# A two-layer decoder trunk: running sums of MLP products kept in PSUM, and per-partition scalings moved from VectorE to ScalarE

## The chip, the cores and the metric

The kernel runs on one core of a Trainium2 chip. The metric is the device time of one execution in microseconds; lower is better. The engines are called PE (TensorE; PEld is its weight load), DVE (VectorE), ACT (ScalarE), POOL (GpSimd) and SP (SyncE, which issues most DMAs).

## The reference

A residual stream x of 256 rows and 2048 columns in f32 goes through two layers. Every sub-layer normalises its input (RMSNorm with a weight per column) and adds its result back. Layer 0 attends with differential attention, layer 1 with latent attention; both then attend to 256 memory tokens and apply a squared-ReLU MLP of width 8192.

```python
def rms_norm(x, g):
    y = xf * lax.rsqrt(jnp.mean(xf * xf, axis=-1, keepdims=True) + EPS)
    return (y * g).astype(x.dtype)

# differential attention, per pair of heads
p = jax.nn.softmax(s, axis=-1)
a = p[:, :, 0] - lam * p[:, :, 1]
o = rms_norm(a @ v, subln) * (1.0 - lambda_init)

# latent attention
d = h @ wdown
c_q  = rms_norm(d[..., :512], q_norm)
c_kv = rms_norm(d[..., 512:1024], kv_norm)
...
# MLP
x = x + jnp.square(jax.nn.relu(rms_norm(x, mlp_norm) @ wup)) @ wdown
```

## The kernel before

**Precision and weights.** Every f32 operand is split into a high part (rounded to the matmul's format) and a low part (the rest), and each product is three matmuls: high x high, high x low, low x high. Weights come from HBM in tiles of 1 MB (`raw`, 7 buffers). ACT casts 128x1024 of it to `whi` (L199), DVE subtracts to get `wlo` (L200); there are four buffers of each, so the splitting runs at most four halves ahead of PE. Activations are split in the same way: `split` (L338, L339) and `halves` (L439, L440).

**Order of the work.** PE's order is written out by hand: the program keeps a clock of PE time, side tasks yield a due time, and their transposes and small matmuls are put between the weight matmuls when they are due. The order of ACT, DVE, POOL and SP comes from a scheduler that works ahead of time with a model of the durations; `urgent()` raises the priority of what it encloses. Each engine then runs its list in that order.

**Norm weights.** A chunk of 512 columns of x is transposed on PE into PSUM (`transpose4`), multiplied by the norm weight of each column, which after the transpose is one scalar per partition and 128-wide piece (`scaled`, L343, and in `Forms.feed`, L451), and split. **Softmax** (`attend4`, `probs`) takes the exponentials on ACT, the reciprocal of the row sums on DVE, and divides on DVE (L622) before PE transposes the rows. **Head norms** of the differential attention (`normed`, L735) scale each head by its inverse root mean square on DVE.

**The MLP's up projection.** For 7 of the 8 blocks of 1024 hidden columns a class `Seven` forms the 2x2 block product with seven products instead of eight. Each product p1 to p7 has two halves (x = 0, 1) of 12 matmuls of 512 columns; the inputs are sums of row blocks of the activations (`sum_of`: s1 to s4, L468) and sums of weight tiles, made on DVE (L824) or by an accumulating DMA on POOL (L816: after p3 has split its tile, POOL's DMA adds the other quarter onto the same tile, which p7 then uses). Each product has a PSUM bank `pr` of its own. Its result is copied (p1 and p5: ACT, L892) or added to earlier ones on DVE (`add`, L886), and four of the seven products finish an output: `out` takes Relu and Square on ACT (L1212, L1213), then PE transposes and `split` stores the hidden unit for the down projection.

**The planner** (`mlp_line`) interleaves the items of `Seven` with items of the other block and of the down projection (24 matmuls each). It keeps the lead of DVE's work over PE's, from costs in `vector` and `tensor`, and takes a product when the lead is not positive. During an MLP only one PSUM bank is left to the side tasks; the down projection's open sums hold four, and the products have what is left.

Of the kernel before, what the change touches and what calls it, by code (L numbers as in the profile page):

```python
# [10 lines left out]
F32 = mybir.dt.float32  # L11
# [3 lines left out]
ALU = mybir.AluOpType  # L15
# [32 lines left out]
def trunk(ctx, tc, x, xT, xT0, mem, memT, positions, gcols, gfinal, lam_vecs, consts, W, out):  # L48
# [100 lines left out]
    def give_back():  # L149
        free_banks[0] += 1  # L150

    def mmul(o, stationary, moving, start, stop):
        n = 1
        for d in moving.shape[1:]:
            n *= d
        clock[0] += max(0.11, n / 2400 + 0.0133)
        return nc.tensor.matmul(o, stationary, moving, start=start, stop=stop)  # L157

    def flip(o, src):
        clock[0] += 0.109  # L160
# [173 lines left out]
    def split(dst, t, src):  # L334
# [3 lines left out]
        nc.scalar.copy(hi, src)  # L338
        nc.vector.tensor_tensor(dst[:, 1, :n, t * P : (t + 1) * P], src, f32(hi), ALU.subtract)  # L339

    def scaled(src, cols):
        tmp = work.tile([P, 4, P], F32, tag="ev", name=nm("xg"), bufs=EVS)
        nc.vector.tensor_tensor(tmp, src, cols.unsqueeze(2).broadcast_to([P, 4, P]), ALU.mult)  # L343
        return tmp

    def transpose4(src, pt):
# [75 lines left out]
    class Forms(Stream):  # L422
# [19 lines left out]
        def feed(self, c, t, ps):  # L442
            xc = xs[t][:, c * CH : (c + 1) * CH]

            def task():
                sum_squares(self.ss[t][:, c : c + 1], xc)
                yield T_ADD
                pt = transpose4(xc, ps)
                rows = self.raw[t][:, 4 * c : 4 * c + 4]
                cols = g[:, self.gcol + 4 * c : self.gcol + 4 * c + 4]  # L450
                nc.vector.tensor_tensor(rows, pt, cols.unsqueeze(2).broadcast_to([P, 4, P]), ALU.mult)  # L451
                self.halves((t, c // 2), c % 2, rows)
                yield T_TURN

            self.form((t, c // 2)).run(task())
# [145 lines left out]
    def attend4(score_pairs, inputs, v, dst, causal, scales=(1.0, 1.0), slack=0.0):  # L601
# [4 lines left out]
        def probs(t, p, nk):  # L606


            sb = yield from side_bank()
            heads = (2 * p, 2 * p + 1)  # L610
            pr = work.tile([P, CH], F32, tag="ev", name=nm("p"), bufs=EVS)[:, : 2 * nk]
            rows = pr.rearrange("p (h k) -> p h k", k=nk)
            if nk == P:
                view = sb.rearrange("p (h a k) -> p h a k", h=2, a=2)
                scores(view, [score_pairs(h, True) for h in heads], t, False)
                nc.vector.tensor_tensor(rows, view[:, :, 1], masks(2), ALU.add)
                nc.vector.tensor_tensor(rows, rows, view[:, :, 0], ALU.add)
                pr, rs = softmax(pr, 2, pr, scales[t])
            else:
                scores(sb.rearrange("p (h k) -> p h k", k=nk), [score_pairs(h, False) for h in heads], t, causal)  # L620
                pr, rs = softmax(sb, 2, pr, scales[t])
            nc.vector.tensor_tensor(rows, rows, rs[:, :2].unsqueeze(2).broadcast_to([P, 2, nk]), ALU.mult)  # L622
            yield T_SM + slack
            nb = nk // P
            for i in range(2 * nb):
                flip(sb[:, i * P : (i + 1) * P], pr[:, i * P : (i + 1) * P])
            src = sb[:, : 2 * nk].rearrange("p (h b q) -> p h b q", h=2, b=nb)
            hi = pTs[p][:, 0, :, :nb, t * P : (t + 1) * P]
            nc.scalar.copy(hi, src)
            nc.vector.tensor_tensor(pTs[p][:, 1, :, :nb, t * P : (t + 1) * P], src, f32(hi), ALU.subtract)  # L630
            give_back()
            yield T_TURN
# [58 lines left out]
    def attend_diff(q, k, v, dst, coef, subcols):  # L691
# [34 lines left out]
        def normed(t, blocks, out):  # L726
            for b in blocks:
                yield b
            po = out[0]
            ss = small.tile([P, 2], F32, tag="ss2", name=nm("ss2"))  # L730
            for h in range(2):
                sum_squares(ss[:, h : h + 1], po[:, h * S : (h + 1) * S])
            r = rsqrt_mean(ss, 2, S)
            os = work.tile([P, CH], F32, tag="ev", name=nm("os"), bufs=EVS)
            nc.vector.tensor_tensor(  # L735
                os.rearrange("p (h d) -> p h d", h=2), po.rearrange("p (h d) -> p h d", h=2),
                r[:, 0:2].unsqueeze(2).broadcast_to([P, 2, S]), ALU.mult,
            )
            yield T_NORM
            split(dst, t, scaled(transpose4(os, po), subcols))  # L740
            give_back()
            yield T_TURN
# [58 lines left out]
    class Seven:  # L801

        ORDER = "p1 p1 p5 p5 p6 p3 p6 p3 p2 p7 p2 p7 p4 p4".split()
        A = {"p1": (0, 0), "p2": (0, 1), "p3": "s4", "p4": (1, 1), "p5": "s1", "p6": "s2", "p7": "s3"}

        def __init__(self, l, b):
# [58 lines left out]
        def products(self, a, u, copied, out):  # L867
            p, x = u
            form = a.form(self.A[p])
            need(form.tasks)  # L870
            if x == 0:
                self.banks[p] = bank("pr")
            o = self.banks[p]
            for h, (hi, lo) in enumerate(take()):
                for k in range(2):
                    kk = 4 * x + 2 * h + k
                    wh, wl = (w[:, k * CH : (k + 1) * CH] for w in (hi, lo))
                    mmul(o, form[:, 0, kk], wh, kk == 0, False)
                    mmul(o, form[:, 0, kk], wl, False, False)
                    mmul(o, form[:, 1, kk], wh, False, kk == 7)  # L880
                pump()
            if x == 0:
                return

            def add(o, p, q, op=ALU.add):
                nc.vector.tensor_tensor(o, p, q, op)  # L886

            c = copied
            if p in ("p1", "p5", "p6", "p3"):
                c[p] = work.tile([P, CH], F32, tag="ev", name=nm(p), bufs=EVS)  # L890
            if p in ("p1", "p5"):
                nc.scalar.copy(c[p], o)  # L892
            elif p == "p6":
                add(c[p], o, c["p1"])
            elif p == "p3":
                add(c[p], o, c["p5"])
                add(c[p], c[p], c["p6"], ALU.subtract)
                out(0, 1, c[p], c[p])
            elif p == "p2":
                add(c["p1"], o, c["p1"])  # L900
                out(0, 0, c["p1"], c["p1"])
            elif p == "p7":
                add(c["p6"], o, c["p6"])
                add(c["p5"], c["p5"], c["p6"], ALU.subtract)
                out(1, 1, c["p5"], c["p5"])
            else:
                add(c["p6"], o, c["p6"])
                out(1, 0, c["p6"], c["p6"])

    def mlp_line(l):  # L910

# [22 lines left out]
        def vector(item):  # L934

            if isinstance(item.of, Seven):
                p, x = item.u
                return 1 + (p in ("p5", "p6", "p2")) + x * {"p6": 0.3, "p3": 0.9, "p2": 0.6, "p7": 0.9, "p4": 0.6}.get(p, 0)
            return 1 + 0.6 * (item.u == len(item.of.all) - 1 and item.of.close)

        def tensor(item):
# [631 lines left out]
```

## Time and profile before

| what | value |
|---|---|
| median of 3 runs | 2216.66 us (2216.47 to 2217.68) |
| span of the profiled execution, first to last instruction | 2214.3 us |
| PE busy | 2201.7 us, 10559 matmuls |
| DVE busy | 1760.7 us, 1961 instructions |
| ACT busy | 1357.0 us, 1811 instructions |
| POOL busy | 134.3 us, 222 instructions |
| granted PE clock | 0.999 |
| HBM | 205 GB/s over the span |

The page gives the profiled execution's span and no other time for it; the span is 2.4 us under the median, and what lies around it (start and end of the execution) is taken to be that. Busy times are sums over the span. The windows give the busy time of each engine in a stretch, the waits name the engine and line on which an engine stood idle, and the chain of waits follows back from the last instruction what released each step.

### The profile page before, as it was taken

Reading aid. Unit: us, or ns where it says so; the run is one execution under the profiler, and the core shown is the slowest. Engines: PE = TensorE matmul, PEld = TensorE weight load, DVE = VectorE, ACT = ScalarE, POOL = GpSimd, SP = SyncE. Lnnn points to the kernel's source line nnn. Section 1 sums busy time; section 2 is a strip of 40 time slices with the busy share of each in tenths; the row PEclk is TensorE's granted clock in tenths of the full one; section 3 lists DMA queues with packets and bytes.
Section 4 is the critical chain, followed back from the end, with each engine's and each line's share of the span. In section 5 each row is a group of like instructions: output and inputs, shape, how many; then the busy total and the mean of one; then the engine's idle time right before and its main releaser. Section 6 shows DMA issues by size and latency. Waiting matters only on the chain.

```text
span 2214.3 us, 27594 instructions
## 1 busy us (share of the span) xinstructions
PE 2201.7 (99%) x10559; PEld 1846.1 (83%) x10559; DVE 1760.7 (80%) x1961; ACT 1357.0 (61%) x1811; POOL 134.3 (6%) x222
## 2 busy tenths in 40 slices
PE   9999999999999999999999999999999999999998
PEld 7888888888888888888889988888888888888886
DVE  6665757779889889889765878778988998898874
ACT  7554546666666666666655755556766666666664
POOL 1111010000000000000000411000000000000001
PEclk9999999999999999999999999999999999999999
DMA  9446555436766766875845444634767667677681
GB/s 386 156 152 228 188 194 210 166 118 209 259 203 211 254 212 215 250 218 212 251 176 178 136 152 163 247 129 156 222 234 228 210 246 228 197 259 226 195 282 57
DMA packets 69683, 454.73 MB, mean 205 GB/s; under 512 B 7984, under 2 KB 8368, under 8 KB 17584
## 3 DMA queue, kind: packets, MB, share of 16 engines
q1 hardware_dynamic: 65232, 423.09, 53.6%
q0 software_dynamic: 4032, 29.36, 7.2%
q8 instruction: 82, 1.34, 0.2%
q10 hardware_dynamic: 288, 0.52, 0.1%
q14 instruction: 49, 0.40, 0.0%
HBM read 450.85 MB, written 2.10 MB: 205 GB/s over the span
## 4 chain that ended last, share of the span: by engine, by line
PE 93%; DVE 4%; issue 1%; ACT 1%; POOL 1%; DMA 1%; POOLq 0%; ACTq 0%; DVEq 0%
PE mm L157 65%; PE pr L157 23%; PE ax L157 2%; PE ax L161 2%; DVE wlo L200 2%; PE mm L161 1%; DVE raw L824 1%; DVE unit L440 0%; DVE raw L468 0%; POOL rs L382 0%; ACT whi L199 0%; DMA raw<-in_mlp_wup_dram 0%; DVE raw L451 0%; DMA raw<-in_da_wqkv_dram 0%; DVE x L496 0%
## 5 line engine op out<-in xcount | busy, mean ns | idle before, releaser
L199 ACT CAST whi<-raw 128x1024 fp32r<-128x1024 f32 (+2 forms) x962 | 1000.4, 1041 | 715.2 <-PE mm L157 590.6
L200 DVE TENSOR_TENSOR wlo<-raw,whi 128x1024 fp32r<-128x1024 f32 (+2 forms) x962 | 1147.8, 1209 | 344.9 <-ACT whi L199 329.6
L157 PE MATMUL mm<-whi,unit 128*128 128x512 f32 (+3 forms) x4416 | 1396.2, 388 | 0.4 <-ACT unit L370 0.4
L157 PEld LDWEIGHTS mm<-whi,unit 128*128 128x128 f32 x4416 | 825.2, 188 | 161.4 <-ACT unit L370 1.5
L157 PE MATMUL mm<-wlo,unit 128*128 128x512 f32 (+3 forms) x2208 | 851.5, 386 | 1.0 <-DVE wlo L200 1.0
L157 PE MATMUL pr<-whi,unit 128*128 128x512 f32 x1568 | 505.6, 391 | 0.0
L157 PEld LDWEIGHTS mm<-wlo,unit 128*128 128x128 f32 x2208 | 415.3, 188 | 79.2 <-DVE wlo L200 3.3
L157 PEld LDWEIGHTS pr<-whi,unit 128*128 128x128 f32 x1568 | 294.4, 188 | 61.0
L157 PE MATMUL pr<-wlo,unit 128*128 128x512 f32 x784 | 305.4, 390 | 0.6 <-DVE wlo L200 0.6
L824 DVE TENSOR_TENSOR raw<-raw,raw 128x2048 f32<-128x2048 f32 x84 | 192.1, 2287 | 26.1 <-DMA raw<-in_mlp_wup_dram 25.6
L157 PEld LDWEIGHTS pr<-wlo,unit 128*128 128x128 f32 x784 | 147.3, 188 | 31.5 <-DVE wlo L200 1.4
L496 DVE TENSOR_TENSOR x<-x,mm 128x512 f32<-128x512 f32 x152 | 100.3, 679 | 9.4 <-PE mm L157 9.0
L816 POOL DMA_DIRECT2D raw<-in_mlp_wup_dram x28 | 24.6, 879 | 1094.7 <-DVE wlo L200 1094.7
L382 POOL TENSOR_TENSOR rs<-rs,mhalf 128x1 f32<-128x1 f32 (+1 forms) x28 | 26.0, 932 | 649.3 <-DVE rs L381 649.3
L338 ACT CAST unit<-ax 128x512 fp32r<-128x512 f32 x64 | 37.2, 581 | 24.4 <-PE ax L161 24.4
L886 DVE TENSOR_TENSOR p<-pr,p 128x512 f32<-128x512 f32 x70 | 47.9, 684 | 2.6 <-PE pr L157 2.6
L157 PE MATMUL mm<-unit,whi 128*128 128x256 f32 x256 | 47.1, 285 | 0.1
L161 PE MATMUL ax<-identr,p 128*128 128x128 f32 x304 | 46.2, 272 | 0.5 <-ACT unit L1434 0.5
L161 PEld LDWEIGHTS ax<-identr,p 128*128 128x128 f32 x304 | 37.7, 139 | 10.8 <-ACT unit L1434 0.9
L1212 ACT ACTIVATE p<-p,r 128x512 f32<-128x512 f32 x56 | 40.3, 720 | 9.3 <-DVE p L886 9.2
L339 DVE TENSOR_TENSOR unit<-ax,unit 128x512 fp32r<-128x512 f32 x64 | 43.7, 683 | 1.6 <-ACT unit L338 1.1
L376 ACT ACTIVATE junk<-x 128x512 bf16<-128x512 f32 x56 | 35.2, 628 | 9.4 <-DVE x L496 8.4
(161 smaller groups left out, 1053.2 us busy)
## 6 DMA issues: line engine op xcount, KB each, us to landing
raw<-in_mlp_wup_dram SPq DMA_DIRECT2D x128, 1024.0 KB, 5.0
raw<-in_mlp_wdown_dram SPq DMA_DIRECT2D x128, 1024.0 KB, 5.1
raw<-in_da_wqkv_dram SPq DMA_DIRECT2D x45, 1024.0 KB, 7.3
raw<-in_mlp_wup_dram POOLq DMA_DIRECT2D x28, 1024.0 KB, 8.1
raw<-in_da_wo_dram SPq DMA_DIRECT2D x16, 1024.0 KB, 5.0
raw<-in_ca_wkv_dram SPq DMA_DIRECT2D x16, 1024.0 KB, 5.0
raw<-in_mla_wo_dram SPq DMA_DIRECT2D x16, 1024.0 KB, 5.2
raw<-in_ca_wq_dram SPq DMA_DIRECT2D x8, 1024.0 KB, 6.9
```

The lines of the kernel that those rows point to most:

```text
L157: return nc.tensor.matmul(o, stationary, moving, start=start, stop=stop)
L161: nc.tensor.transpose(o, src, ident)
L199: nc.scalar.copy(hi, r)
L200: nc.vector.tensor_tensor(lo, r, f32(hi), ALU.subtract)
L338: nc.scalar.copy(hi, src)
L339: nc.vector.tensor_tensor(dst[:, 1, :n, t * P : (t + 1) * P], src, f32(hi), ALU.subtract)
L376: nc.scalar.activation(junk[:, : src.shape[1]], src, AF.Square, accum_out=acc)
L382: nc.gpsimd.tensor_tensor(r[:, :n], r[:, :n], mhalf.broadcast_to([P, n]), ALU.pow)
L496: nc.vector.tensor_tensor(xc, xc, ps, ALU.add)
L824: nc.vector.tensor_tensor(o, o, q, ALU.add)
L886: nc.vector.tensor_tensor(o, p, q, op)
L1212: nc.scalar.activation(r, src, AF.Relu, scale=rstd[t])
```

## The change

Four things are changed. First, `Seven`'s products share banks: p6, p7 and p4 accumulate onto the bank of p1, p3 onto that of p5; p2 keeps its own. The running sums p1, p1+p6 and p5 are copied by ACT (`kept`, urgent) on the way; three subtractions or additions per block are left on DVE, and p4's output is read by Relu straight from the bank. The order of the fourteen half products swaps p2's second half with p7's second half, and the planner's costs of DVE work are lowered. Second, norm weights are applied by ACT in four pieces of 128 columns (`gained`). Third, softmax rows are divided by ACT, a piece per head. Fourth, head norms are applied by ACT, a piece of 256 columns per head.

```diff
-    def mmul(o, stationary, moving, start, stop):
+    def mmul(o, stationary, moving, start, stop, onto=False):
...
-        return nc.tensor.matmul(o, stationary, moving, start=start, stop=stop)
+        return nc.tensor.matmul(o, stationary, moving, start=start, stop=stop, skip_group_check=onto)
...
+    def gained(dst, src, cols):
+        for k in range(4):
+            nc.scalar.activation(dst[:, k], src[:, k], AF.Copy, scale=cols[:, k : k + 1])
+
     def scaled(src, cols):
         tmp = work.tile([P, 4, P], F32, tag="ev", name=nm("xg"), bufs=EVS)
-        nc.vector.tensor_tensor(tmp, src, cols.unsqueeze(2).broadcast_to([P, 4, P]), ALU.mult)
+        gained(tmp, src, cols)
         return tmp
...
-                nc.vector.tensor_tensor(rows, pt, cols.unsqueeze(2).broadcast_to([P, 4, P]), ALU.mult)
+                gained(rows, pt, cols)
...
-            nc.vector.tensor_tensor(rows, rows, rs[:, :2].unsqueeze(2).broadcast_to([P, 2, nk]), ALU.mult)
+            for i in range(2):
+                nc.scalar.activation(rows[:, i], rows[:, i], AF.Copy, scale=rs[:, i : i + 1])
...
-            nc.vector.tensor_tensor(
-                os.rearrange("p (h d) -> p h d", h=2), po.rearrange("p (h d) -> p h d", h=2),
-                r[:, 0:2].unsqueeze(2).broadcast_to([P, 2, S]), ALU.mult,
-            )
+            for h in range(2):
+                nc.scalar.activation(os[:, h * S : (h + 1) * S], po[:, h * S : (h + 1) * S], AF.Copy, scale=r[:, h : h + 1])
...
-        ORDER = "p1 p1 p5 p5 p6 p3 p6 p3 p2 p7 p2 p7 p4 p4".split()
+        ORDER = "p1 p1 p5 p5 p6 p3 p6 p3 p2 p7 p7 p2 p4 p4".split()
+        ONTO = {"p1": "p1", "p6": "p1", "p7": "p1", "p4": "p1", "p5": "p5", "p3": "p5", "p2": "p2"}
...
-            if x == 0:
+            onto = self.ONTO[p]
+            if x == 0 and onto == p:
                 self.banks[p] = bank("pr")
-            o = self.banks[p]
+            o = self.banks[onto]
...
-                    mmul(o, form[:, 0, kk], wh, kk == 0, False)
-                    mmul(o, form[:, 0, kk], wl, False, False)
-                    mmul(o, form[:, 1, kk], wh, False, kk == 7)
+                    mmul(o, form[:, 0, kk], wh, kk == 0 and onto == p, False, onto != p)
+                    mmul(o, form[:, 0, kk], wl, False, False, onto != p)
+                    mmul(o, form[:, 1, kk], wh, False, kk == 7, onto != p)
...
-            def add(o, p, q, op=ALU.add):
-                nc.vector.tensor_tensor(o, p, q, op)
+            def kept():
+                t = work.tile([P, CH], F32, tag="ev", name=nm(p), bufs=EVS)
+                with urgent():
+                    nc.scalar.copy(t, o)
+                return t
...
-            if p in ("p1", "p5", "p6", "p3"):
-                c[p] = work.tile([P, CH], F32, tag="ev", name=nm(p), bufs=EVS)
-            if p in ("p1", "p5"):
-                nc.scalar.copy(c[p], o)
-            elif p == "p6":
-                add(c[p], o, c["p1"])
+            if p in ("p1", "p5", "p6"):
+                c[p] = kept()
             elif p == "p3":
-                add(c[p], o, c["p5"])
-                add(c[p], c[p], c["p6"], ALU.subtract)
-                out(0, 1, c[p], c[p])
+                nc.vector.tensor_tensor(c["p6"], o, c["p6"], ALU.subtract)
+                out(0, 1, c["p6"], c["p6"])
+            elif p == "p7":
+                with urgent():
+                    nc.vector.tensor_tensor(c["p5"], c["p5"], o, ALU.subtract)
+                out(1, 1, c["p5"], c["p5"])
             elif p == "p2":
-                add(c["p1"], o, c["p1"])
+                nc.vector.tensor_tensor(c["p1"], o, c["p1"], ALU.add)
                 out(0, 0, c["p1"], c["p1"])
-            elif p == "p7":
-                add(c["p6"], o, c["p6"])
-                add(c["p5"], c["p5"], c["p6"], ALU.subtract)
-                out(1, 1, c["p5"], c["p5"])
             else:
-                add(c["p6"], o, c["p6"])
-                out(1, 0, c["p6"], c["p6"])
+                out(1, 0, o, work.tile([P, CH], F32, tag="ev", name=nm(p), bufs=EVS))
...
-                return 1 + (p in ("p5", "p6", "p2")) + x * {"p6": 0.3, "p3": 0.9, "p2": 0.6, "p7": 0.9, "p4": 0.6}.get(p, 0)
+                return 1 + (p in ("p5", "p6", "p2")) + x * {"p3": 0.6, "p2": 0.6, "p7": 0.6, "p4": 0.3}.get(p, 0)
```

## The prediction

> **What bounds the kernel now.** I read the page first, then the table by windows of 40 us, the waits of TensorE (PE) and the groups by line; for single places the chain of waits and the timeline. The page's first two lines:
>
> ```profile
> span 2214.3 us, 27594 instructions
> PE 2201.7 (99%) x10559; PEld 1846.1 (83%) x10559; DVE 1760.7 (80%) x1961; ACT 1357.0 (61%) x1811; POOL 134.3 (6%) x222
> ```
>
> PE is busy 99% of the span. Because matmuls overlap, "busy" could hide slack, so I compare the issue rate in a covered stretch of the chain with a matmul's own length in the groups by form:
>
> ```profile
> 665.01 10.88 PE mm L157 x48
> L157 PE MATMUL mm<-whi,unit 128*128 128x512 f32 x4160 | 1337.1, 392 | 0.4 <-ACT unit L370 0.4
> ```
>
> 48 matmuls in 10.88 us are 0.227 us each; one lasts 0.392. So a late operand shows as idle time only after 0.165 us of it. Next, where PE is not busy at all (columns: window, length, then busy us and count for PE, PEld, DVE, ACT, POOL; granted clock, DMA share, GB/s) and for whom it waited (total us, times, longest):
>
> ```profile
> 0.00:40.00 40.00, 38.37 (x158) 28.83 (x159) 28.63 (x59) 29.00 (x50) 0.76 (x5) 1.00 0.98 373
> 520.00:560.00 40.00, 39.71 (x179) 32.35 (x178) 37.45 (x33) 26.53 (x31) 1.91 (x2) 1.00 0.69 213
> ...
> 1280.00:1320.00 40.00, 39.48 (x247) 35.20 (x246) 31.31 (x50) 22.77 (x41) 2.19 (x5) 1.00 0.49 171
> ...
> 1640.00:1680.00 40.00, 39.60 (x177) 32.44 (x176) 36.24 (x30) 25.98 (x29) 1.74 (x2) 1.00 0.63 188
> ...
> 2200.00:2240.00 40.00, 5.54 (x25) 4.26 (x23) 4.29 (x10) 4.12 (x8) 1.10 (x2) 0.90 0.15 53
> ```
>
> ```profile
> PE mm L157 <- DVE wlo L200: 1.0, 3, 0.4
> PE pr L157 <- DVE wlo L200: 0.6, 2, 0.3
> PE ax L161 <- ACT unit L1434: 0.5, 1, 0.5
> ```
>
> 1.6 us of idle lie in the first window, 8.8 us behind the last matmul; the change touches neither. Between them seven windows (the first and last stand above) are short by 2.2 us together, nearly all in the six waits named. With 0.165 us hidden in each of seven, **all that PE loses in the middle is about 3.3 us**. That is the most that any relief of another engine can return: 0.15% of the span. A measurement of this kernel can tell about 0.2%, or 4.4 us, from no change.
>
> **The change part by part.** The matmuls keep their number, sizes and operands; four products now start without clearing the bank. So PE's 2201.7 us stay, and the question is which operands come later or sooner. The work that moves, from the groups by line:
>
> ```profile
> L199 ACT CAST whi<-raw 128x1024 fp32r<-128x1024 f32 (+2 forms) x962 | 1000.4, 1041 | 715.2 <-PE mm L157 590.6
> L200 DVE TENSOR_TENSOR wlo<-raw,whi 128x1024 fp32r<-128x1024 f32 (+2 forms) x962 | 1147.8, 1209 | 344.9 <-ACT whi L199 329.6
> L886 DVE TENSOR_TENSOR p<-pr,p 128x512 f32<-128x512 f32 x70 | 47.9, 684 | 2.6 <-PE pr L157 2.6
> L886 DVE TENSOR_TENSOR p<-p,p 128x512 f32<-128x512 f32 x28 | 19.1, 683 | 0.0
> L892 ACT COPY p<-pr 128x512 f32<-128x512 f32 x28 | 16.1, 575 | 0.0
> L343 DVE TENSOR_TENSOR xg<-mm,g 128x512 f32<-128x512 f32 x24 | 15.6, 686 | 6.4 <-PE mm L161 6.4
> ...
> L343 DVE TENSOR_TENSOR xg<-ax,g 128x512 f32<-128x512 f32 x4 | 2.6, 684 | 0.1
> L451 DVE TENSOR_TENSOR raw<-mm,g 128x512 f32<-128x512 f32 x16 | 10.3, 684 | 3.3 <-PE mm L161 3.3
> L622 DVE TENSOR_TENSOR p<-p,rsum 128x512 f32<-128x512 f32 (+1 forms) x24 | 14.4, 608 | 0.0
> L735 DVE TENSOR_TENSOR os<-ax,rs 128x512 f32<-128x512 f32 x8 | 5.5, 688 | 4.7 <-POOL rs L382 4.7
> ```
>
> Off VectorE (DVE): the 98 additions of L886 shrink to 3 per block, 42 in the 14 blocks, so 56 x 0.684 = 38.3 us; the norm weights (36 of L343 in three groups, 16 of L451) 52 x 0.686 = 35.7; divisions 14.4; head norms 5.5. Together 93.9 us: DVE falls to about 1667 us.
>
> Onto ScalarE (ACT): the nearest rows for a scaled copy out of PSUM in pieces are the latent rows' evacuations:
>
> ```profile
> 1204.81 0.73 ACT L1325 ACTIVATE lat<-mm,r 128x128 f32<-128x128 f32 x2 [0.31 <-PE mm L157]
> 1219.99 0.47 ACT L1325 ACTIVATE lat<-mm,r 128x256 f32<-128x256 f32 x1
> ```
>
> Two pieces of 128 take 0.73 us, so four take up to 1.46, against 0.686 on DVE; two of 256 at most 0.94. So 52 x 1.46 = 76 us; divisions 16 x 0.94 + 8 x 0.73 = 21; head norms 8 x 0.94 = 7.5; one copy more per block (p6), 14 x 0.575 = 8. About 112 us: ACT rises to 1470 us, 66%. Neither engine becomes the bound on average; only bursts and latencies count.
>
> [...]
>
> *The new bank waits.* p6, p7 and p4 pile onto p1's bank, p3 onto p5's, so each must wait until the sum so far has been read. I worked the planner's rule through with its new costs: from the second block on, each block reads p1 p1' p5 D p5' D p6 D p3 p6' D p3' p2 D D p7 p7' p2' D D p4 p4' (a dash: second half; D: an item of the down projection). At 0.227 us a matmul, a product item is 2.7 us and D 5.4. Between the end of p5' and p3 lie D, p6, D; between p7' and p4 lie p2', D, D: 13.6 us each; the other two gaps are longer. The reader needs 0.575 us (copy) or 0.684 (subtraction). Cost: nothing, hidden by those items; uncovered it would be their length, 56 x about 0.6 = 34 us.
>
> *Latent layer, kv latent.* Here DVE's weighting goes to an ACT that is full:
>
> ```profile
> 1224.12 1.29 DVE L343 TENSOR_TENSOR xg<-ax,g 128x512 f32<-128x512 f32 x2
> 1226.28 1.17 ACT L338 CAST unit<-xg 128x512 fp32r<-128x512 f32 x2
> 1228.78 1.83 DVE L339 TENSOR_TENSOR unit<-xg,unit 128x512 fp32r<-128x512 f32 x2
> PEld mm L157 <- DVE unit L339: 0.3, 1, 0.3
> ```
>
> The unit's casts end at 1227.45 and PE already waits for the low halves, done at 1230.61. Two weightings add 2.9 us to ACT; if all goes in front, the casts end at 1230.4, the two low halves (1.4 to 1.8) at about 1232: +1.3. If ACT lets a weight cast of 1.05 pass later, +0.3. I take **+1.0**.
>
> *Divisions.* They put 0.7 to 0.9 us on ACT for 0.6 on DVE. In the latent heads DVE is the late one too:
>
> ```profile
> 1292.60 0.67 DVE L622 TENSOR_TENSOR p<-p,rsum 128x512 f32<-128x512 f32 x1
> 1293.42 0.63 PE L161 MATMUL ax<-identr,p 128*128 128x128 f32 x4 [0.52 <-ACT unit L1434]
> ```
>
> The wait of 0.52 is put down to ACT's L1434, but what waits are transposes of probabilities, and this division, held up in DVE's queue, ends only at 1293.27. Bounds -0.7 (it goes) to +4 (one us in each of four head groups); I take **0**, as the two engines are about equally full there (31.3 and 22.8 of 40 us).
>
> *First block's accumulating DMA.* In block 1 the new order is p3' p2 p7 p7' with nothing between. p7' reads the raw tile that POOL's DMA sums onto after p3':
>
> ```profile
> 554.77 0.68 DVE L886 TENSOR_TENSOR p<-pr,p 128x512 f32<-128x512 f32 x1
> 555.37 2.35 DVE L200 TENSOR_TENSOR wlo<-raw,whi 128x1024 fp32r<-128x1024 f32 x2
> 556.90 0.87 POOL L816 DMA_DIRECT2D raw<-in_mlp_wup_dram  x1 [10.22 <-DVE wlo L200]
> raw<-in_mlp_wup_dram POOLq DMA_DIRECT2D x28, 1024.0 KB, 8.1
> DMA to landing us min/median/max: 2.6/5.0/14.4
> 563.43 4.13 PE pr L157 x18
> ```
>
> It lands at 565.0; cast 1.04 and low half 1.21 make it 567.2. PE starts p7 at 563.43 (last row), ends it 2.72 later at 566.15, and needs the low half of p7' 0.23 after that: 0.8 us late. Behind the waiting cast on ACT stand the next casts and the Relu of p3's result, which nothing needs for some 10 us. The addition at 554.77 goes, which pulls the DMA 0.6 forward. I take 0.5 in each layer, **+1.0**; bounds 0, and 6 each at the longest landing of any DMA. In later blocks D, D lie between: nothing. What moves with the swap of p2' and p7': the load of p2' on SP and its addition L824 come one item later, and p7' gives its raw tile back one to four items sooner, so no load finds fewer free tiles; POOL's DMA keeps its place.
>
> *Relief of DVE bursts.* Why PE waits at 614:
>
> ```profile
> 607.12 0.68 DVE L886 TENSOR_TENSOR p<-pr,p 128x512 f32<-128x512 f32 x1
> 611.53 2.29 DVE L824 TENSOR_TENSOR raw<-raw,raw 128x2048 f32<-128x2048 f32 x1
> 613.74 4.62 DVE L200 TENSOR_TENSOR wlo<-raw,whi 128x1024 fp32r<-128x1024 f32 x4
> 490.00:500.00 10.00, 10.00 (x50) 8.34 (x49) 10.00 (x14) 6.49 (x11) 0.00 (x0) 1.00 0.41 137
> ```
>
> The wait of 0.4 (0.57 with the hidden part) is shorter than the addition at 607.12, which goes; twice, -1.1. At the entry of each MLP DVE is full from 490 on (last row) and loses eight weightings, 5.5 us: the wait of 0.3 (0.45) goes, twice, -0.9. What is late next is a weight's cast on ACT, which has about 3.5 us idle in that window. One wait near 820 follows a DMA and stays. Sum -2.0, bounds -2.5 and +3.
>
> *Sum.* +1.0 + 0 + 1.0 - 2.0 = 0.0. The profiled execution shows 2214.3 us from first to last instruction; the median of the runs is 2216.66, the 2.4 around it being start and end. So the span stays near 2214 and the time near **2216.5**.
>
> **The rivals.**
>
> *Only the relief (0.18).* All 3.3 us return and nothing new is late: 2213.4. For it: DVE is named in five of six waits. Against it: the kv latent already waits, and ACT is full there.
>
> *ScalarE's queue (0.20): slower.* Its added pieces stand in front of weight casts and low-half work. Place: the latent layer's four head groups, the kv latent, the two MLP entries. Price: four softmaxes of 0.9 us per group, half seen by PE, 4 x 1.7 = 6.8; kv 1.3; entries: two pairs of weightings in 490 to 500 add 5.8 us against 3.5 idle, half of the 2.3 seen, at two entries 2.3; relief of 2.0 kept: +8.4, 2225.1. It decides once ACT's backlog exceeds the weights that lie ahead, four halves of 1.36 us (5.4) in a run of products. For it: the row at 1226.28; against it: 34% of ACT stays idle. [...]
>
> *The accumulating DMA (0.14).* Landing 3 us later than the median, at both layers: 2 x 3.3 extra, 2222 to 2223. It speaks for it that the margin is negative already; against, that DVE is freed just before.
>
> *Faster by more than 4.4 us (0.04).* Needs more than PE's idle time in the middle; only the edges hold it, and nothing there changes.
>
> **How the numbers follow.** The forecast has 0.44: 2216.5, its own range 2214 to 2220. The range runs from 2213.2 (full relief) to 2225 (most of the ScalarE rival); outside lie the fourth rival and about half the second, some 0.15. Faster by over 0.2%: 0.04. Slower: most of the second, over half of the third, a little of the forecast: 0.28. Within: 0.68.
>
> **What would show it.** Right: PE busy again about 2202 us; L886 with 42 additions; ACT near 1460 and DVE near 1670 us; no PE wait on ACT's p copies; the wait near 614 gone; PE waiting 1 to 1.5 us on the kv unit's low half, and up to 1 us on a low half in block 1. Wrong: waits on whi (L199) in the latent heads or MLP entries, a p7' wait of several us, or the p copies among PE's waits.

## The result, and the profile after

| kernel | median | runs |
|---|---|---|
| before | 2216.66 us | 2215.57 to 2217.68, 5 runs |
| after | 2227.37 us | 2221.98 to 2228.94, 5 runs |

The medians lie 10.7 us apart, and 2227.37 is above the upper end of the range (2225.0). The ratio over all runs is 1.0042, 95% interval [1.0031, 1.0053], or 9.4 us, which is also the difference of the means (2226.1 against 2216.7). The profiled execution of after has a span of 2227.2 us against 2214.3, so 12.9 us more. The runs of after lie up to 7 us apart, those of before 2 us. The granted clock, averaged over each run of after, goes with it: 0.996 at 2228.94 us, 0.999 at 2221.98, and the other three between or level with the first. A difference of 0.003 is some 13 us at half clock and so about 6.7 us of time, an estimate.

The page of after, its first two lines:

```profile
span 2227.2 us, 27718 instructions
PE 2208.3 (99%) x10559; PEld 1852.1 (83%) x10559; DVE 1688.6 (76%) x1821; ACT 1433.1 (64%) x2097; POOL 133.8 (6%) x222
```

The same 10559 matmuls are busy for 6.6 us more (2208.3 against 2201.7), and PE's idle time is 18.9 us against 12.6, so 6.3 more. The two add up to the 12.9. Neither DVE nor ACT has become the bound.

The idle part is found in the waits of PE in after (total us, times, longest):

```profile
PE pr L157 <- DVE wlo L200: 4.3, 2, 2.2
PE ax L161 <- ACT p L627: 2.7, 2, 2.0
PE mm L157 <- DVE unit L339: 1.4, 1, 1.4
```

These 8.4 us of idle time are new. The six waits of before that the prediction named, 2.1 us, are gone, which leaves the 6.3. The three lines are the low halves of a product (first MLP block of each layer), the divided probabilities of the latent heads, and the kv latent.

The busy part is found with the windows of after, cut at the starts of the stretches with a lower clock (window, length, busy us and count for PE, PEld, DVE, ACT, POOL; granted clock, DMA share, GB/s):

```profile
566.72:570.14 3.42, 1.24 (x8) 0.83 (x7) 3.42 (x3) 2.68 (x4) 0.00 (x0) 1.00 0.46 192
570.14:573.55 3.41, 3.41 (x9) 2.65 (x10) 3.41 (x4) 1.05 (x1) 0.00 (x0) 0.50 0.80 250
1232.32:1235.74 3.42, 1.94 (x14) 1.50 (x14) 3.42 (x5) 3.12 (x7) 3.34 (x5) 1.00 0.30 117
1235.74:1239.15 3.41, 3.41 (x18) 3.41 (x18) 1.78 (x3) 0.33 (x2) 2.96 (x5) 0.50 0.47 125
1396.16:1399.58 3.42, 1.41 (x8) 0.73 (x7) 3.42 (x9) 3.42 (x8) 0.00 (x0) 1.00 0.00 0
1399.58:1402.99 3.41, 3.41 (x12) 2.73 (x12) 0.98 (x2) 1.45 (x4) 0.00 (x0) 0.50 0.77 228
1614.62:1618.03 3.41, 1.32 (x6) 1.05 (x6) 3.41 (x4) 1.62 (x3) 0.00 (x0) 1.00 0.29 50
1618.03:1621.45 3.42, 3.42 (x9) 2.45 (x8) 3.42 (x5) 1.05 (x1) 0.00 (x0) 0.50 0.90 323
```

Each odd row holds a wait; in each even row, right after it, **PE was granted half its clock for 3.41 us**: in the first, 9 matmuls of 512 columns where 3.41 / 0.227 = 15 would fit. By the granted clock of 0.50 a stretch costs about 3.41 / 2 = 1.7 us, an estimate, and four of them 6.8; the busy time rose by 6.6. A wait of about 2 us was thus paid nearly twice, and the second payment is not in the table of waits.

How the first of these waits arises, which ends at 569.96, is shown by the chain of waits of after (start, us, what) and, under it, by DVE's timeline:

```profile
558.22 1.24 DVE wlo L200
...
559.47 6.99 DMA raw<-in_mlp_wup_dram
...
566.48 0.04 DVE raw L828
...
568.69 1.23 DVE wlo L200
...
569.96 2.37 PE pr L157 x5
```

```profile
564.17 1.23 DVE L200 TENSOR_TENSOR wlo<-raw,whi 128x1024 fp32r<-128x1024 f32 x1 [1.35 <-ACT whi L199]
566.48 2.29 DVE L828 TENSOR_TENSOR raw<-raw,raw 128x2048 f32<-128x2048 f32 x1 [1.09 <-DMA raw<-in_mlp_wup_dram]
568.69 1.22 DVE L200 TENSOR_TENSOR wlo<-raw,whi 128x1024 fp32r<-128x1024 f32 x1
```

The low half that PE waits for is the last row. Ahead of it in DVE's list stands L828, the sum of weight tiles that belongs to p2's second half, and DVE stands still for it: its tile's load went out at 559.47, when a raw buffer came free, and landed at 566.46. The low half's own input was there earlier:

```profile
554.80 0.87 POOL L820 DMA_DIRECT2D raw<-in_mlp_wup_dram  x1 [8.70 <-DVE wlo L200]
563.08 1.05 ACT L199 CAST whi<-raw 128x1024 fp32r<-128x1024 f32 x1 [1.28 <-DMA raw<-in_mlp_wup_dram]
```

These rows, of POOL and ACT in after, are the accumulating DMA and the cast of p7's second half, done at 564.13. Without the addition ahead of it DVE would have made the low half at 565.40, when it fell idle, and been done at 566.6; PE's last matmul before the wait starts at 567.3. In before the same sum stands eight low halves earlier in DVE's list, and its tile was there:

```profile
550.30 2.28 DVE L824 TENSOR_TENSOR raw<-raw,raw 128x2048 f32<-128x2048 f32 x1
```

### The profile page after: what moved, and what is told of

Its sections match the earlier page's. It is cut to its first block, busy times and chain, and to the rows that moved or that the text cites. A ratio compares the mean times of both kernels' runs of the same rounds, so it can differ in the third digit from the quotient of the medians.

```text
span 2227.2 us, 27718 instructions
## 1 busy us (share of the span) xinstructions
PE 2208.3 (99%) x10559; PEld 1852.1 (83%) x10559; DVE 1688.6 (76%) x1821; ACT 1433.1 (64%) x2097; POOL 133.8 (6%) x222
## 4 chain that ended last, share of the span: by engine, by line
PE 97%; ACT 1%; DMA 1%; DVE 0%; issue 0%; ACTq 0%; POOLq 0%; DVEq 0%
PE mm L157 68%; PE pr L157 23%; PE ax L157 3%; PE ax L161 2%; PE mm L161 1%; DMA raw<-in_mlp_wup_dram 1%; ACT whi L199 0%; DVE wlo L200 0%; ACT p L565 0%; DMA raw<-in_da_wqkv_dram 0%; ACT xg L343 0%; ACT unit L374 0%; ACT junk L380 0%; ACT p L627 0%; ACT raw L634 0%
## 5 line engine op out<-in xcount | busy, mean ns | idle before, releaser
L828 DVE TENSOR_TENSOR raw<-raw,raw 128x2048 f32<-128x2048 f32 x84 | 192.3, 2289 | 41.1 <-DMA raw<-in_mlp_wup_dram 41.0
L339 DVE TENSOR_TENSOR unit<-ax,unit 128x512 fp32r<-128x512 f32 x64 | 44.0, 687 | 0.4
L157 PEld LDWEIGHTS mm<-unit,whi 128*128 128x128 f32 x256 | 41.2, 198 | 2.0 <-DVE unit L339 1.6
L339 DVE TENSOR_TENSOR unit<-xg,unit 128x512 fp32r<-128x512 f32 x36 | 24.9, 705 | 18.9 <-ACT unit L338 18.9
```

Source lines behind the costliest of these rows:

```text
L828: nc.vector.tensor_tensor(o, o, q, ALU.add)
```

## The experiments

Theory 1: three places make the loss (low halves of the first block, divisions on ACT, kv weights on ACT), each with the half-clock stretch behind it. Rivals are told with each run. All ratios are against before, measured on the same chip; intervals are 95%. The size of a part is given as a difference of means from after (2226.1), because after's five runs lie so far apart; by the medians it would be about 1.1 to 1.5 us more each.

**Divisions back on DVE.**

```diff
-            for i in range(2):
-                nc.scalar.activation(rows[:, i], rows[:, i], AF.Copy, scale=rs[:, i : i + 1])
+            nc.vector.tensor_tensor(rows, rows, rs[:, :2].unsqueeze(2).broadcast_to([P, 2, nk]), ALU.mult)
```

> The changed kernel with the softmax divisions back on VectorE. Theory 1: the two waits of PE's transposes on ACT p (2.7 us idle, 3 with what is hidden) and one half-clock stretch (1.7 us) go: about -4.8 us, near 2222.5 us. Theory 2: ACT loses 20 of its added 76 us of work, so at most a quarter of the slowdown goes, -2.5 us, near 2225.

Measured: 2222.82 us, ratio 1.0029 [1.0018, 1.0040]; 3.1 us under after. This interval overlaps that of after, so the time alone doesn't settle it; PE's waits do: those on p (2.7 us) are gone, those of the first blocks and of the kv latent are still there. Why ACT was late, the chain of after shows:

```profile
1392.48 0.94 ACT whi L199
1393.42 0.27 ACT raw L634
1393.69 2.06 ACT p L565 x8
1395.74 1.20 ACT unit L374 x3
1396.94 0.94 ACT whi L199
1397.88 0.41 ACT unit L374
1398.29 0.47 ACT raw L634
1398.76 0.31 ACT p L627
```

Between the divisions of one group and those of the next, on ACT, stand 6.3 us of casts, exponentials and splits. The exponentials end at 1395.75; the division behind them ends at 1399.07, and PE starts at 1399.12.

**The latents' norm weights back on DVE** (`True`: one multiplication of 512 columns, as before).

```diff
-            split(dst, t, scaled(transpose4(es[t], b), g[:, gcol : gcol + 4]))
+            split(dst, t, scaled(transpose4(es[t], b), g[:, gcol : gcol + 4], True))
```

> The changed kernel with the norm weights of the two latents alone (four weightings) back on VectorE. Theory 1: the wait of PE on the kv unit's low half (1.4 us idle, 1.9 with the next) falls back to about 0.3 and its half-clock stretch (1.7 us) goes: about -3.3 us, near 2224. Theory 2: ACT loses 5 us of 76, so under 1 us.

Measured: 2224.01 us, ratio 1.0033 [1.0021, 1.0045]; 2.3 us under after, again with overlapping intervals. The wait on `unit` L339 (1.4 us) is gone from the list; the waits on p and on the first blocks' low halves stay.

**p2's addition left out in the first block of each layer** (its tile is loaded, but not summed, so p4 of that block uses other data).

```diff
-                    add(r["t", x], o)
+                    if (self.b, x) != (SEVEN[0], 1):
+                        add(r["t", x], o)
```

> The changed kernel without one weight addition on VectorE (2.29 us): that of p2's second half in the first block of each layer is left out, so p4's weights lack a term there. Every transfer, the accumulating one too, stays. Theory 1a (the first block's stall of 2.4 us is this addition: it stands in VectorE's list ahead of p7's low half and waits there for the tile that SP loads): both waits of PE pr on wlo go, about -5 us of idle and up to two half-clock stretches of 1.7, so 2219 to 2222 us. Theory 1b (the accumulating DMA lands too late for p7's second half): the waits stay, 2227.

Measured: 2220.14 us, ratio 1.0017 [1.0008, 1.0027]; 6.1 us under after, and its interval lies clear of after's. PE's waits on product low halves are gone, though the accumulating DMA and the order are those of after. That refutes the DMA and shows the addition as the cause. The three undone parts sum to 3.1 + 2.3 + 6.1 = 11.5 us; 2226.1 - 11.5 = 2214.6, near the 2213.4 that before would take without its 3.3 us of old waits. So little else is lost.

**The old order and the old planner costs.**

```diff
-        ORDER = "p1 p1 p5 p5 p6 p3 p6 p3 p2 p7 p7 p2 p4 p4".split()
+        ORDER = "p1 p1 p5 p5 p6 p3 p6 p3 p2 p7 p2 p7 p4 p4".split()
...
-                return 1 + (p in ("p5", "p6", "p2")) + x * {"p3": 0.6, "p2": 0.6, "p7": 0.6, "p4": 0.3}.get(p, 0)
+                return 1 + (p in ("p5", "p6", "p2")) + x * {"p6": 0.3, "p3": 0.9, "p2": 0.6, "p7": 0.9, "p4": 0.6}.get(p, 0)
```

> The changed kernel with the old order of the half products (p2 p7 p2 p7) and the old planner costs; all else as changed. Theory 1 (the slowdown is four places at which PE stands idle for 1.7 to 2.4 us and then runs at half clock for 3.4 us; two of them come from the swapped order in the first block of each layer): both waits of PE pr on DVE wlo (4.3 us) and two of the four half-clock stretches go, about -8.4 us, so near 2219 us. Theory 2 (ScalarE's longer queue delays weight casts everywhere): the order is not the cause, the time stays within 2 us of 2227.

Measured: 2235.09 us, ratio 1.0080 [1.0063, 1.0097]: a miss, and in the other direction. The first blocks' waits went, but blocks 2 to 4 of each layer got one each:

```profile
PE mm L157 <- DVE wlo L200: 11.0, 7, 2.5
```

So the swap of p2 and p7 makes the stall of the first block, but undoing it only moves the stall to other blocks.

**All three together: old order and costs, divisions and latents' weights on DVE.**

> All three together: old order and planner costs, softmax divisions and the latents' norm weights on VectorE; the sums in PSUM, the other norm weights and the head norms as changed. Theory 1: none of the four stalls is left and the reliefs of VectorE stay, so 2213 to 2215 us, 2 to 3 us under the kernel before. Theory 2: ScalarE still has some 55 us more than before, so still above 2221.

Measured: 2228.56 us, ratio 1.0054 [1.0039, 1.0069]: a miss. Six waits of 1.3 to 2.4 us in the same blocks; the chain and DVE's timeline at the first show the mechanism of the first block again:

```profile
643.58 7.65 DMA raw<-in_mlp_wup_dram
```

```profile
651.26 2.29 DVE L830 TENSOR_TENSOR raw<-raw,raw 128x2048 f32<-128x2048 f32 x1 [4.61 <-DMA raw<-in_mlp_wup_dram]
```

**The sums in PSUM alone**: every scaling back on DVE, old order and costs.

```diff
-        for k in range(4):
-            nc.scalar.activation(dst[:, k], src[:, k], AF.Copy, scale=cols[:, k : k + 1])
+        nc.vector.tensor_tensor(dst, src, cols.unsqueeze(2).broadcast_to([P, 4, P]), ALU.mult)
...
```

> The products share banks as in the changed kernel, in the old order and with the old planner costs; all scalings are on DVE again. Theory A (the sums in PSUM alone take about 38 us of additions off DVE, so the scheduler places the additions of weight tiles earlier, where they wait for their tile and hold up the low halves behind them): stalls of 1.5 to 2.6 us in blocks 2 to 4 of the layers stay, and the run lies near the kernel with old order, divisions and latents' weights on DVE: 2224 to 2230. Rival B (it takes the norm weights on ScalarE in the MLP's norms to fill ScalarE, the sums in PSUM alone are harmless): no stalls over 1 us, 2214 to 2217.

Measured: 2230.71 us, ratio 1.0059 [1.0044, 1.0074], 0.7 us above the range of theory A, with the six waits that it named. In this profiled run and in that of the run above no half-clock stretch came before the last matmul (granted clock 0.999 in each), and both are the fastest of their four (2225.94 here and 2225.74). The groups by line of DVE have the additions in one row each, with the idle time before them and what ended it: before, after, this kernel, and the next one (ScalarE's pieces alone).

```profile
L824 DVE TENSOR_TENSOR raw<-raw,raw 128x2048 f32<-128x2048 f32 x84 | 192.1, 2287 | 26.1 <-DMA raw<-in_mlp_wup_dram 25.6
```

```profile
L828 DVE TENSOR_TENSOR raw<-raw,raw 128x2048 f32<-128x2048 f32 x84 | 192.3, 2289 | 41.1 <-DMA raw<-in_mlp_wup_dram 41.0
```

```profile
L828 DVE TENSOR_TENSOR raw<-raw,raw 128x2048 f32<-128x2048 f32 x84 | 192.1, 2287 | 46.6 <-DMA raw<-in_mlp_wup_dram 46.3
```

```profile
L827 DVE TENSOR_TENSOR raw<-raw,raw 128x2048 f32<-128x2048 f32 x84 | 192.2, 2288 | 23.7 <-DMA raw<-in_mlp_wup_dram 23.1
```

With the sums in PSUM DVE stands longer before the additions; with the scalings moved, it does not. DVE's lists show why. PE works through the same list in before, in this kernel and in the next. Of the 84 additions, 16 stand one low half earlier in DVE's list here than in before, the six ahead of PE's waits among them; with ScalarE's pieces alone it is 2 of 84. One of the six, in before and here:

```profile
651.78 2.29 DVE L824 TENSOR_TENSOR raw<-raw,raw 128x2048 f32<-128x2048 f32 x1 [1.24 <-DMA raw<-in_mlp_wup_dram]
```

```profile
651.54 2.29 DVE L828 TENSOR_TENSOR raw<-raw,raw 128x2048 f32<-128x2048 f32 x1 [3.69 <-DMA raw<-in_mlp_wup_dram]
```

The tile comes at about the same time in both. In before DVE makes one more low half at 649.32 while it waits; here that low half stands behind the addition. How empty DVE is in all does not decide it: it is busy for 1760.7 us in before, 1733.3 here, and 1718.3 with ScalarE's pieces alone.

**ScalarE's pieces alone**: before, with the norm weights, divisions and head norms on ACT.

> The kernel before with the norm weights, divisions and head norms on ScalarE in pieces, but the products, their banks, their order and the planner as before. Theory 1: the stalls at the kv latent (1.9 us) and the latent heads (about 3.5 us) and one or two half-clock stretches are there, the first-block stalls are not: 2216.4 + 5.4 + 1.7 to 3.4 - 1 to 2 of relief = about 2222 to 2224. If the products alone made the kernel slow it would be near 2216.

Measured: 2220.77 us, ratio 1.0018 [1.0009, 1.0028], a little under what was expected; its profiled execution had the waits on p (2.7) and `unit` (1.4) and no half-clock stretch (granted clock 0.999). No wait of a first block, and none over 0.4 us on a low half.

**PE made to wait on purpose**: before, with nine pauses of different length, made by a chain of small products on POOL between two transposes.

> The kernel before with nine pauses made for PE: it transposes the identity, ScalarE copies it, GpSimd multiplies it by itself 0 to 5 times, PE transposes the result, which nothing uses. The profile then shows idle times of PE of about 1 to 5 us, and for each whether matmuls after it run at half clock. Theory (a PE idle of about 2 us or more within a fixed grid of 3.4 us halves the clock for one 3.4 us stretch): no half clock after idles up to 1 us, always after 4 us or more, either way for 1.5 to 2.5 us. Rival (every idle above a threshold costs): a sharp limit between two lengths.

Measured: 2258.76 us in one run. The pauses among PE's waits:

```profile
PE ax L161 <- POOL probe L1294: 26.2, 8, 4.7
...
PE ax L161 <- ACT probe L1292: 0.5, 1, 0.5
```

Seven of the nine were followed by a half clock (granted clock over the run 0.993); the shortest (0.5 us) and one of 2.60 us were not. That one lies in PE's timeline between 378.70 + 0.27 and 381.57; another of the same length, between 435.56 + 0.27 and 438.43, was followed by half clock:

```profile
381.57 0.33 PE L161 MATMUL ax<-identr,probe 128*128 128x128 f32 x1 [2.60 <-POOL probe L1294]
```

```profile
438.43 0.48 PE L161 MATMUL ax<-identr,probe 128*128 128x128 f32 x1 [2.60 <-POOL probe L1294]
```

The windows of this kernel are cut at multiples of 3.4133 us from the starts of the half-clock stretches. The step is taken from after: three of its stretches start 665.60, 829.44 and 1047.89 us behind the first, which are 195, 243 and 307 steps of 3.4133.

```profile
376.90:380.31 3.41, 2.07 (x10) 1.44 (x8) 1.56 (x2) 1.54 (x3) 0.13 (x1) 1.00 1.04 440
380.31:383.73 3.42, 2.16 (x12) 1.86 (x13) 0.89 (x1) 0.00 (x0) 1.20 (x1) 1.00 0.81 259
383.73:387.14 3.41, 3.41 (x16) 2.77 (x16) 2.29 (x3) 1.67 (x2) 0.00 (x0) 1.00 0.48 197
393.96:397.37 3.41, 0.78 (x4) 0.70 (x5) 1.23 (x1) 1.22 (x3) 1.20 (x2) 1.00 0.37 82
397.37:400.79 3.42, 3.42 (x10) 2.65 (x9) 0.00 (x0) 0.00 (x0) 0.00 (x0) 0.50 0.68 271
434.92:438.33 3.41, 0.91 (x5) 0.47 (x3) 2.75 (x6) 1.21 (x2) 1.90 (x2) 1.00 0.41 171
438.33:441.75 3.42, 3.32 (x9) 2.65 (x10) 0.00 (x0) 0.00 (x0) 0.04 (x1) 0.50 0.78 254
```

The two half-clock stretches in these rows start at 397.37 and 438.33, 40.96 us or 12 steps apart. The first pause of 2.60 us is shared by two windows, busy for 2.07 and 2.16 us, and the clock stays; the second lies in one window, busy for 0.91, and the next window runs at half clock, as it does after the window busy for 0.78. So the length of the wait alone did not decide; in these rows it went with how much of one window of a fixed grid PE was busy. The waits of 1.4 to 3.2 us ahead of these two and of after's four each lay mostly in one window, busy for 0.78 to 1.94 us.

**The changed kernel with the old order and its new planner costs.** By the planner's rule p7' then stands directly ahead of p4 in blocks 3 to 7 of each layer, so that the wait for the reader of the shared bank has nothing to hide it.

> The changed kernel with the old order of the half products and its new planner costs. In blocks 3 to 7 of each layer p7' then stands directly ahead of p4 (ten places), so p4 must wait for the subtraction that reads the shared bank after p7'. If a bank wait costs about its reader plus a hand-over: 0.9 to 1.2 us in each of ten places, PE waits on DVE's p among its waits with 8 to 10 us in total; the first-block stalls (2.3 us each) go, kv latent and heads as in the changed kernel. In all 2224 to 2232. Rival (PE's sequencer or the halves ahead hide the reader): no such wait, 2217 to 2221.

Measured: 2246.49 us, ratio 1.0133 [1.0117, 1.0148], 14 us beyond the expected. Waits and one place of DVE's timeline:

```profile
PE pr L157 <- DVE p L904: 18.5, 10, 1.9
```

```profile
767.25 0.68 DVE L339 TENSOR_TENSOR unit<-ax,unit 128x512 fp32r<-128x512 f32 x1
767.85 0.68 DVE L904 TENSOR_TENSOR p<-p,pr 128x512 f32<-128x512 f32 x1
```

Ten waits, as many as the rule gives, but 1.9 us each and not 0.9 to 1.2: the urgent subtraction still came behind the low half of a unit on DVE (first row). Four of the ten have a half-clock stretch behind them (granted clock of the profiled run 0.995). The new order hides all of this: with it, after is 19 us faster.

**A mixed version**: after, with divisions and latents' weights on DVE and the old order in the first block of each layer only.

```diff
+        FIRST = "p1 p1 p5 p5 p6 p3 p6 p3 p2 p7 p2 p7 p4 p4".split()
...
+            names = self.FIRST if self.b == SEVEN[0] else self.ORDER
```

> The changed kernel with divisions and the latents' norm weights on VectorE and with the old order of half products in the first block of each layer alone; planner costs and the other six blocks as changed. By the planner's rule the first block then has four down items between p2' and p7', and the other blocks two between p3' and p7. Theory 1: none of the stalls is left, 2213 to 2215 us. If the additions' waits turn up elsewhere, as with the old order in all blocks (stalls of 1.5 to 2.6 us in blocks 2 to 4), about 2 us for each.

Measured: 2214.81 us in 10 runs (2213.34 to 2216.08) against 2216.60 in 25, ratio 0.9990 [0.9981, 1.0000]: the fastest of all, by about 0.1% with an interval that reaches none; its mean is 2214.6, what the three parts gave. No half-clock stretch before the end (granted clock 0.999); one wait is left, at 1696, where the chain and DVE's timeline have

```profile
1684.58 9.68 DMA raw<-in_mlp_wup_dram
```

```profile
1694.28 2.29 DVE L831 TENSOR_TENSOR raw<-raw,raw 128x2048 f32<-128x2048 f32 x1 [5.51 <-DMA raw<-in_mlp_wup_dram]
```

**The mixed version, with p2's addition made by POOL's DMA.**

```diff
-                    add(r["t", x], o)
+                    self.fetch(1, 0, x, r["t", x])
```

> The best version so far (the changed kernel with divisions and latents' weights on DVE and the old order in the first blocks; 2214.8) with p2's addition taken off DVE: POOL's DMA fetches that quarter from HBM a second time and adds it onto the tile (28 MB more traffic, 28 x 2.29 = 64 us less on DVE). Theory (the addition in DVE's list that waits for its tile makes the stalls): the stall of 1.7 us near 1695 goes, DVE falls to about 1637 us, no PE wait on a low half of a product over 1 us; 2212 to 2215. Rival (DVE, emptied further, places the other additions earlier still, or the DMA's traffic delays the loads): new stalls on low halves or on raw tiles, 2217 to 2225.

Measured: 2252.23 us, ratio 1.0164 [1.0148, 1.0179]: the rival, and 27 us beyond its range. Instead of one wait on a low half there are eleven, as below; two more, 4.1 us together, are on the reader of the shared bank (`p` L908), and seven half-clock stretches come on top (granted clock 0.994):

```profile
PE mm L157 <- DVE wlo L200: 21.6, 11, 2.4
```

In the chain at one of them, near 680, a load took 10.29 us, and the addition behind it, one of the 56 left on DVE, waited 4.5 us with a low half behind it. How much of that is the extra traffic and how much the emptier DVE list, this run does not separate.

**The mixed version, with p2's addition on POOL's own arithmetic.**

```diff
-                    add(r["t", x], o)
+                    nc.gpsimd.tensor_tensor(r["t", x], r["t", x], o, ALU.add)
```

> The same version with p2's addition on POOL, which waits for the tile there instead of in DVE's list. Theory: the stall near 1695 goes and DVE falls by 64 us, as with the DMA; 2212 to 2215. Rival (POOL works 4 to 8 us on a tile and slows DVE beside it, or holds up its accumulating DMAs): waits on low halves or on the DMA's tile, 2217 to 2230.

Measured: 2228.43 us, ratio 1.0051 [1.0034, 1.0068]: the rival again. DVE hardly waits for a load any more (1.0 us before the additions), but one piece of the chain and POOL's timeline beside it show a new price:

```profile
540.67 5.53 DVE wlo L200
```

```profile
540.18 4.92 POOL L861 TENSOR_TENSOR raw<-raw,raw 128x2048 f32<-128x2048 f32 x1 [34.67 <-DMA raw<-in_mlp_wup_dram]
```

A low half of 1.2 us took 5.5 and ended 1.1 after POOL had finished; PE then waited 1.0 us. Beside POOL's next addition, 4.58 us from 551.47 on, it came dearer: a low half of 5.64 us, a wait of 2.5 and a half-clock stretch. Both happen in each layer (PE's waits on low halves 7.6 us in seven, granted clock 0.997). What in POOL's addition holds up the low half is not shown.

## Why the prediction was right or wrong

**What bounds the kernel.** Right: PE did, and the 3.3 us of old waits were all that could come back. Most of it did: with the three faults undone, what is left is about 2215 us (2214.6 by the parts and by the mixed version, where one wait of 1.7 remains), near the rival "only the relief" (2213.4). The work that moved was less than the sum had it: DVE's busy time fell by 72 us, not 94, and ACT's rose by 76, not 112; the forecast's sum of terms doesn't use either.

**The sums in PSUM.** No bank wait at all in after, as worked out from the planner's rule. The price for the uncovered case was too low: 1.9 us a place, not 0.6, because the reader waits its turn on DVE.

**First block, forecast at +1.0 for both layers: the step that failed.** Measured 4.3 us of idle time and, in the profiled run, two half-clock stretches; 6.1 us by the run without the additions. The DMA that the step weighed landed in time: it went out at 554.80 (556.90 in before) and was there by 563.08. The failing sentence is the one on the swap: the load of p2' and its addition come later, "so no load finds fewer free tiles". It counted raw buffers and didn't ask where the addition stands in DVE's list, nor what is queued behind it when its tile is late. There the sum stands eight low halves later in DVE's list than in before, because p2' now comes behind p7', and just ahead of the low half that p7' needs. With the old order the stall moves to other blocks, for the opposite reason: there 16 additions stand one low half earlier. DVE's idle time before the additions agrees: 38 to 50 us in every version with sums in PSUM and all its additions on DVE, 23 to 26 without. Why the scheduler, which works ahead with a model of the durations, draws them forward is not shown; a plausible reason is that the sums in PSUM take work out of DVE's list right beside them, while the scalings that moved lie mostly elsewhere.

**Divisions, forecast at 0: the second step that failed.** The bounds (-0.7 to +4) held 2.7 of idle time; the value taken was too low, and with the half-clock stretch of the profiled run (4.4) it lies outside them. "About equally full" was an average over 40 us, and 31.3 against 22.8 is not even equal; what counted were the 6.3 us that stand between the divisions of two groups on ACT. The rival of ScalarE's queue had the mechanism and, in the heads, two of four groups.

**kv latent, forecast at +1.0.** Right in place, cause and, without the clock, size: PE waited 1.4 us, where in before its weight load had waited 0.3. A weight cast did get between the two unit casts, and the eight pieces were cheaper than their bound, 2.19 us on ACT's timeline in after:

```profile
1227.87 2.19 ACT L343 ACTIVATE xg<-ax,g 128x128 f32<-128x128 f32 x8
1230.68 0.71 ACT L338 CAST unit<-xg 128x512 fp32r<-128x512 f32 x1
1231.21 1.14 ACT L199 CAST whi<-raw 128x1024 fp32r<-128x1024 f32 x1
1232.15 0.71 ACT L338 CAST unit<-xg 128x512 fp32r<-128x512 f32 x1
```

That is 1.1 us for four, against the 1.46 that was taken.

**The missing term.** The sum had only idle time in it. In the profiled run of after, four half-clock stretches of 1.7 us are half of the loss, and no step allowed for them, since before has none ahead of its last matmul. With the idle times as they came out but without the clock, the span would have been 2220.6 and the time about 2222, inside the range; after's run with a granted clock of 0.999 has a span of 2220.2 and took 2221.98.

**What would show it.** Of the signs named, right were: additions down to 42, DVE near 1670 (1689) and ACT near 1460 (1433) in direction, no wait on p copies, the wait near 614 gone, 1 to 1.5 us on the kv unit. Wrong: PE busy "again about 2202" (2208.3), which is the clock's mark, and "up to 1 us" in block 1 (2.2).

## What to carry to other kernels

Taking work off an engine that isn't the bound, or swapping items on another, can shift instructions in its list: before doing it, look for instructions there that wait for a transfer, and for what stands behind them. To a wait of PE like those that a half clock followed in the rows here (1.4 to 3.2 us) add the 1.7 us that such a stretch can cost, an estimate; when PE's busy time rises with the same matmuls, look for windows with a granted clock of 0.50. An engine's share over 40 us doesn't say whether a short step on a chain finds its turn; read the list of the engine between the two ends of the chain.

## What the runs showed of the hardware

- Ahead of after's last matmul the half clock came in four stretches of 3.41 us that start on a grid of 3.4133 us (195, 243 and 307 steps behind the first), each right after a window of the grid in which PE was little busy; the two read in the kernel with pauses lie 12 steps apart. In after, from 10 us after the start to the last matmul, five windows had under 2.9 us of busy time: those with 1.24, 1.32, 1.41 and 1.94 were followed by one at half clock, that with 2.72 was not. In the kernel with pauses 0.78 and 0.91 were, 2.07 and 2.16 were not. With the latents' weights on DVE a window of 1.67 us (1611.47 to 1614.88) was not either, so the runs show no single limit.
- Where the grid lies against the kernel differs between the profiles: counted from the first instruction, the starts lie 0.11 us behind a multiple of the step in after and 1.42 in the kernel with pauses. Behind the longest wait on p (2.0 us) and the one on `unit` (1.4) after had a half-clock stretch each; ScalarE's pieces alone had the same waits and none, at a granted clock of 0.999. This fits the scatter of after's runs, whose granted clocks go from 0.996 to 0.999.
- A tensor addition of 128x2048 took 2.29 us on DVE (84 in after) and 4.93 on POOL (mean of 28 in the last kernel); there a low half, 1.22 us in the median, took 5.53 and 5.64 beside two of POOL's.
- Loads of 1 MB that DVE's additions waited for took 6.7 to 10.3 us in the chains of waits (6.73 with the sums in PSUM alone, 6.99 in after, 7.65 with all three together, 9.68 in the mixed version, 10.29 with POOL's DMA), against a median of 5.0 for SP's 128 loads of that weight in after.
